# Split-precision products: high and low activations as one 512-wide moving operand, a PSUM bank per output chunk

## The chip, the core and the metric

The kernel runs on one core of one Trainium2 chip. The metric is device time in microseconds (us) of one execution. The kernel before takes 1823.14 us (median of three runs, 1821.18 to 1823.35).

## What is computed

The reference runs a stack of layers on x, 256 tokens by 1024 features, in float32. Two hybrid layers come first; each has five branches (stick-breaking attention, a matrix LSTM, spatial gating, retention, attention over a memory) that are projected up, gated and merged. Then come a recurrent mixer, a conformer convolution, two cross-attentions and two convolutional feed-forward blocks (FFN). What matters here is that nearly all the arithmetic is products of activations with large weight matrices that are read once from HBM:

```python
h = rms_norm(x, norm_pre)
proj = h @ w_in
...
h = rms_norm_2(x, norm) @ w_up
g = causal_dwconv(h[..., :D_FF], dw_w, dw_b)
u = h[..., D_FF:]
return (jax.nn.gelu(g) * u) @ w_down
```

The results have to be accurate to float32, while TensorE multiplies in a reduced format at full rate. So each operand is split into a high and a low part, and a product is the sum of three: high by high, high by low, low by high.

## The kernel before, in words

**Layout.** Most activations stand with features on the 128 partitions and the 256 tokens along the free axis; `xF` holds x as 8 chunks of 128 features. Other tensors stand with tokens on partitions ("row-major" below: `mm_T`, `proj_T`, `T_plain`, tile `psT`).

**Weights.** `weights` (L281) reads a block of weights as tiles `raw` of 1024 elements a partition, issued on SP's queue. ScalarE (ACT) writes the high part `wh` (L297), VectorE (DVE) the low part `wl` as raw minus high (L298). There are 5 buffers for `raw` and 4 for each split part, so the splits can run at most four tiles ahead of TensorE (PE). The two splits are given a priority ahead of the program order (`AHEAD`), and a scheduler writes out one fixed order for each engine. Every engine works through its order and waits where an operand or a buffer is missing.

**Products with features on partitions.** `Operand` (L244) holds the activations as two tiles, `h` and `l`. `mm_F` (L301) takes a block of 512 by 512 weights, and for each chunk of 128 outputs and each of four steps of 128 inputs it issues three matmuls of 256 columns, all into the same half of a PSUM bank:

```python
for n, (a, b) in enumerate(((wh, xh), (wh, xl), (wl, xh))):
    PE.matmul(pss[m // 2][:, m % 2], a, b,
```

`proj_F` (L328) makes 512 outputs of 1024 inputs with two such calls, into two banks of two chunks each. `scaled_F` (L344) then evicts a bank with one DVE multiplication by the row of reciprocal norms (`rb`), 512 elements wide:

```python
V.tensor_tensor(dst[:, 2 * i:2 * i + 2], pss[i], bc(rb, 2), op=ALU.mult)
```

The output products (tile `psO`) of the mixer, the conformer and the cross-attentions use four banks for all 8 chunks. The loop over input blocks is outside, that over the two column blocks of 512 inside, and `add_to_x` (L937) adds a bank to `xF` and makes the next stage's operand from it. Each hybrid layer's `w_out` product does the same and evicts through ACT (L878). The FFN's down product, `down` in `conv_ffn`, runs `mm_F` too.

**PSUM.** The pool `mm` has four banks for products, `aux` four for everything else; from its second block of 512 features on, the FFN's up projections take theirs from `aux`. Banks are handed out in turn, and a product waits until the bank's former contents have been read.

**Row-major products.** `mm_T` (L313) uses the activations as stationary operand and 512 columns of weights as moving one, again three matmuls a step.

Of the kernel before, what the change touches and what calls it, by code (L numbers as in the profile page):

```python
# [54 lines left out]
def stack_kernel(ctx: ExitStack, tc: tile.TileContext, I: dict, out: bass.AP):  # L55
# [245 lines left out]

    def mm_F(pss, src, op, k0, n_k, first, last):

        w = made.pop() if made else weights(src, n_k)
# [39 lines left out]
    def scaled_F(pss, rb, dst):  # L344

        for i in range(2):
            V.tensor_tensor(dst[:, 2 * i:2 * i + 2], pss[i], bc(rb, 2), op=ALU.mult)

    def F_plain(w, c0, op, rb, name, dst=None, pss=None):
        if pss is None:  # L350
            pss = proj_F(w, c0, op)
        if dst is None:
            dst = t_f4([128, 4, S], name)
        scaled_F(pss, rb, dst)
        return dst
# [9 lines left out]
    def silu2_F(w, c0, op, rb, name, pss=None):  # L365

        z = F_plain(w, c0, op, rb, name, pss=pss)
# [115 lines left out]
    def layer(l, nrm, early, kv, late, nxt):  # L483
# [3 lines left out]
        pss_q = proj_F(w, OFF["sb_q"], op)  # L487
        stage("layer")
        rc, row = nrm.column(), []
        pss_k = proj_F(w, OFF["sb_k"], op, mid=lambda: row.append(row_of(rc, "x")))  # L490
# [25 lines left out]
        def sb_branch():  # L516
            qF = F_plain(w, OFF["sb_q"], op, rb, "sbq", pss=pss_q)
            kF = F_plain(w, OFF["sb_k"], op, rb, "sbk", pss=pss_k)
# [36 lines left out]
            pss_z = proj_F(w, OFF["sb_z"], op, mid=later)  # L555
            z = silu2_F(w, OFF["sb_z"], op, rb, "sbz", pss=pss_z)
# [145 lines left out]
        def rt_branch():  # L702
# [5 lines left out]
            def rot(c0, name):  # L708
                pss = proj_F(w, c0, op)
                q = t_f4([128, 4, S], name)  # L710
                x = t_f4([128, 4, S], name + "_x")
                for i in range(2):
                    sl = slice(2 * i, 2 * i + 2)
                    V.tensor_tensor(q[:, sl], pss[i], bc(cr, 2), op=ALU.mult)
                    V.tensor_tensor(x[0:64, sl], pss[i][64:128], bc(sr[64:128], 2), op=ALU.mult)
                    V.tensor_tensor(x[64:128, sl], pss[i][0:64], bc(sr[0:64], 2), op=ALU.mult)
# [149 lines left out]
        pss = [[mbank([128, 2, S], "psO") for _ in range(2)] for _ in range(2)]  # L866
        for dh in range(2):
            for cg in range(2):
                mm_F(pss[cg], wo[dh * 512:dh * 512 + 512, cg * 512:cg * 512 + 512], mos[dh], 0, 4,
                     dh == 0, dh == 1)  # L870
        oF = [t_f4([128, 4, S], "oF") for _ in range(2)]
        sq = Sq()
        for cg in range(2):
            for i in range(2):
                sl = slice(2 * i, 2 * i + 2)
                for j in range(2):
                    c = 4 * cg + 2 * i + j
                    A.activation(oF[cg][:, 2 * i + j], pss[cg][i][:, j], AF.Copy,  # L878
                                 scale=col("norm_post", l * 8 + c))
                sq.add(pss[cg][i])  # L880
# [56 lines left out]
    def add_to_x(pss, nn, bias=None):  # L937
        for c2 in range(4):
            sl = slice(2 * c2, 2 * c2 + 2)
            ps = pss[c2 // 2][c2 % 2]  # L940
            if bias is None:
                V.tensor_tensor(xF[:, sl], xF[:, sl], ps, op=ALU.add)
            else:
                for j in range(2):
                    c = 2 * c2 + j
                    V.scalar_tensor_tensor(xF[:, c], ps[:, j], col(bias, c), xF[:, c],
                                           op0=ALU.add, op1=ALU.add)
            nn.pair(c2)
        return nn
# [17 lines left out]
    def mixer_ab(nrm, fill_1, fill_2, nxt):  # L967
# [3 lines left out]
        firsts = [proj_F(w, D, op)]  # L971
        rc, row = nrm.column(), []
        firsts.append(proj_F(w, D + 512, op, mid=lambda: row.append(row_of(rc, "x"))))
# [6 lines left out]
        def recurrence(g4):  # L980
            zr = F_plain(w, D + g4 * 512, op, rb, "a_zr", pss=firsts[g4])
# [39 lines left out]
        pss = proj_F(w, 2 * D, op)  # L1021
# [4 lines left out]
        up = t_f6([128, 4, 16 + S], "b_u")  # L1026
        G.memset(up[:, :, 0:16], 0.0)
        for i in range(2):
            V.tensor_tensor(up[:, 2 * i:2 * i + 2, 16:16 + S], pss[i], bc(rb, 2), op=ALU.mult)
# [32 lines left out]
        wo = I["ab_w_out_2"][0]  # L1062
        pss = out_banks()
        for n, (o, r0) in enumerate(((yb, D), (yas[0], 0), (yas[1], 512))):
            for cg in range(2):
                mm_F(pss[cg], wo[r0:r0 + 512, cg * 512:cg * 512 + 512], o, 0, 4, n == 0, n == 2)
        return add_to_x(pss, Norm(*nxt))

    def conformer(nrm, fill_1, fill_2, nxt):
# [3 lines left out]
        first = proj_F(w1, D, op, n=256)[0]  # L1073
# [337 lines left out]
```

## Time and profile before

| what | value |
|---|---|
| median of three runs | 1823.14 us |
| profiled execution | 1826.32 us |
| its span, first to last instruction | 1824.6 us |
| PE busy, matmuls | 1788.9 us (98%) |
| DVE busy | 1265.6 us (69%) |
| ACT busy | 958.9 us (53%) |
| mean granted TensorE clock | 0.993 |
| mean HBM traffic | 169 GB/s |

The profiled execution takes 1826.32 us, 1.7 us more than its span, and is 3.2 us above the median of the runs. In rows by group, the number after x is the count; after the bar come busy time in us, the mean of one in ns, and the engine's idle time just before such instructions with what ended it. In rows by window, the stretch and its length are followed by the busy time and count of PE, PEld (weight loads), DVE, ACT and POOL, then the granted clock as a share of full speed, the busy share of the DMA engines and GB/s. Timeline rows give the start, the duration, the engine and line, and in brackets the idle time before. In the rows of DMA queues the numbers are packets, MB and the share of 16 engines' time. A matmul's own duration includes its way through the array, and successive ones overlap, so rates are read from the distance between starts.

### The profile page before, as it was taken

The page shows a single profiled execution, that of the slowest core. Times are in us where ns is not written, and L with a number is a line of the kernel's source. Part 1 is how long each engine was busy: PE and PEld are TensorE (multiplying, and loading weights), DVE is VectorE, ACT ScalarE, POOL GpSimd, SP SyncE. Part 2 cuts the span into 40 slices and gives each one's busy share as a digit, 9 for nine tenths or more (in the row PEclk, how much of TensorE's full clock was granted, in tenths as well). Part 3 has the DMA queues.
Part 4 walks back from the last instruction along what each step waited for, and adds up shares of the span by engine and source line. Part 5 has one row for each costly group of instructions (what it writes and reads, how often), then busy time and mean ns, then how long its engine had stood idle before and what let it go on. Part 6 is the DMA issues. An engine that isn't in the chain of part 4 may idle for free. (4 is left out here: it accounts for less than half of the span.)

```text
span 1824.6 us, 30483 instructions
## 1 busy us (share of the span) xinstructions
PE 1788.9 (98%) x12255; PEld 1666.0 (91%) x12255; DVE 1265.6 (69%) x1888; ACT 958.9 (53%) x1369; POOL 60.8 (3%) x91
## 2 busy tenths in 40 slices
PE   8899999999999999999999999999999989999998
PEld 8889998888999898888899998999999989899998
DVE  6587856676667877656657965676669985577666
ACT  5755335554556443455455854455457545455443
POOL 0000001100000100000000000000000000000000
PEclk9999999999999999999999999999999999999999
DMA  7456554666554655467655554455554344355552
GB/s 222 131 167 208 168 174 147 202 206 193 165 173 146 185 176 169 149 197 232 207 169 178 156 169 144 155 181 178 183 183 146 103 133 151 116 180 184 183 184 93
DMA packets 162654, 309.57 MB, mean 170 GB/s; under 512 B 10852, under 2 KB 19504, under 8 KB 162512
## 3 DMA queue, kind: packets, MB, share of 16 engines
q1 hardware_dynamic: 159872, 302.04, 52.7%
q0 software_dynamic: 2128, 5.37, 1.0%
q8 instruction: 96, 1.57, 0.4%
q14 instruction: 46, 0.38, 0.1%
q10 hardware_dynamic: 512, 0.21, 0.1%
HBM read 306.53 MB, written 1.05 MB: 169 GB/s over the span
## 5 line engine op out<-in xcount | busy, mean ns | idle before, releaser
L298 DVE TENSOR_TENSOR wl<-raw,wh 128x1024 fp32r<-128x1024 f32 x558 | 668.6, 1222 | 343.8 <-ACT wh L297 335.4
L297 ACT ACTIVATE wh<-raw 128x1024 fp32r<-128x1024 f32 x558 | 573.2, 1054 | 529.9 <-PE psF L310 178.4
L310 PE MATMUL psF<-xh,wh 128*128 128x256 f32 x1888 | 538.4, 285 | 3.5 <-ACT wh L1302 3.3
L310 PE MATMUL psF<-xh,wl 128*128 128x256 f32 x1888 | 536.1, 284 | 0.8 <-DVE wl L298 0.8
L310 PE MATMUL psF<-xl,wh 128*128 128x256 f32 x1888 | 536.7, 284 | 0.0
L310 PEld LDWEIGHTS psF<-xh,wh 128*128 128x128 f32 x1888 | 363.7, 193 | 4.5 <-ACT wh L1302 3.6
L310 PEld LDWEIGHTS psF<-xl,wh 128*128 128x128 f32 x1888 | 364.0, 193 | 1.5 <-issue 1.0
L310 PEld LDWEIGHTS psF<-xh,wl 128*128 128x128 f32 x1888 | 363.3, 193 | 1.6 <-DVE wl L298 1.4
L310 PE MATMUL psO<-yh,wh 128*128 128x256 f32 x800 | 227.6, 285 | 6.0 <-ACT yh L253 6.0
L310 PE MATMUL psO<-yl,wh 128*128 128x256 f32 x800 | 227.3, 284 | 0.0
L310 PE MATMUL psO<-yh,wl 128*128 128x256 f32 x800 | 227.0, 284 | 0.3 <-DVE wl L298 0.3
L323 PE MATMUL psT<-wl,xh 128*128 128x512 f32 x544 | 216.3, 398 | 0.0
L323 PE MATMUL psT<-wh,xl 128*128 128x512 f32 x544 | 216.0, 397 | 0.0
L323 PE MATMUL psT<-wh,xh 128*128 128x512 f32 x544 | 214.5, 394 | 0.0
L310 PEld LDWEIGHTS psO<-yh,wh 128*128 128x128 f32 x800 | 154.2, 193 | 6.9 <-ACT yh L253 6.7
L310 PEld LDWEIGHTS psO<-yh,wl 128*128 128x128 f32 x800 | 154.3, 193 | 0.5 <-DVE wl L298 0.5
L310 PEld LDWEIGHTS psO<-yl,wh 128*128 128x128 f32 x800 | 154.3, 193 | 0.3
L323 PEld LDWEIGHTS psT<-wl,xh 128*128 128x128 f32 x544 | 102.7, 189 | 21.4
L323 PEld LDWEIGHTS psT<-wh,xl 128*128 128x128 f32 x544 | 102.8, 189 | 20.8
L323 PEld LDWEIGHTS psT<-wh,xh 128*128 128x128 f32 x544 | 102.8, 189 | 19.6
L1114 DVE SCALAR_TENSOR_TENSOR c_h<-c_a,cols,c_h 128x229 f32<-128x229 f32 (+15 forms) x144 | 63.2, 465 | 3.0
L323 PE MATMUL psT<-wl,yh 128*128 128x512 f32 x160 | 62.3, 389 | 0.0
(414 smaller groups left out, 2134.0 us busy)
## 6 DMA issues: line engine op xcount, KB each, us to landing
raw<-in_w_in SPq DMA_DIRECT2D x224, 512.0 KB, 4.3
raw<-in_f_w_up SPq DMA_DIRECT2D x96, 512.0 KB, 4.3
raw<-in_f_w_down SPq DMA_DIRECT2D x48, 512.0 KB, 4.3
raw<-in_w_up SPq DMA_DIRECT2D x40, 512.0 KB, 4.0
raw<-in_c_w_pw SPq DMA_DIRECT2D x24, 512.0 KB, 3.9
raw<-in_ab_w_in SPq DMA_DIRECT2D x20, 512.0 KB, 4.4
raw<-in_w_mem_kv SPq DMA_DIRECT2D x16, 512.0 KB, 3.9
raw<-in_w_out SPq DMA_DIRECT2D x16, 512.0 KB, 3.6
```

The source lines that it names most:

```text
L297: A.activation(hi, raw, AF.Copy)
L298: V.tensor_tensor(lo, raw, hi.bitcast(F32), op=ALU.subtract)
L310: PE.matmul(pss[m // 2][:, m % 2], a, b, start=(first and m % 2 == 0 and k == 0 and n == 0), stop=(last and k == n_k - 1 and n == 2), skip ...
L323: PE.matmul(pss[t], a, b, start=(first and k == 0 and n == 0), stop=(last and k == n_k - 1 and n == 2), skip_group_check=True)
L1114: V.scalar_tensor_tensor(h[:, j:], a[:, m, 0:S - j], col("c_dw_w_2", (30 - j) * 8 + c), h[:, j:], op0=ALU.mult, op1=ALU.add)
```

## The change

**Operand.** High and low parts stand side by side in one tile `hl`; `h` and `l` are views of it. `mm_P`, new, takes a block of 512 inputs by 256 outputs. For each step it issues two matmuls in place of three: the high weights against high and low activations as one moving operand of 512 columns, which fills a bank, and the low weights against the high activations, 256 columns added to the bank's first half. A bank holds one chunk of 128 outputs, and its halves are added at eviction.

**Eviction.** `join` copies the first half to SBUF on ACT and adds the second on DVE. `proj_F` makes its outputs by columns, 256 at a time over all 1024 inputs, and returns an SBUF tile; the multiplication by `rb` then reads and writes that tile. `proj_out` makes the output products in two halves of 512 columns, four banks each, and hands on two chunks at a time; `out_to_x` adds both halves of a bank to `xF` by two DVE instructions a chunk. `mm_F` stays for the FFN's down product alone. The weight tiles of the changed products are 4 by 256 elements a partition in place of 2 by 512: the same count and size, with runs of 1 KB in place of 2 KB.

```diff
-            self.h = pool.tile([128, n, S], F32R, tag=tag + "h", name=tag + "h")
-            self.l = pool.tile([128, n, S], F32R, tag=tag + "l", name=tag + "l")
+            self.hl = pool.tile([128, n, 2, S], F32R, tag=tag + "hl", name=tag + "hl")
+            self.h, self.l = self.hl[:, :, 0], self.hl[:, :, 1]
...
+    def mm_P(pss, src, op, k0, n_k, first, last):
+
+        w = made.pop() if made else weights(src, n_k)
+        for m in range(src.shape[1] // 128):
+            for k in range(n_k):
+                wh, wl = w[k][0][:, m * 128:m * 128 + 128], w[k][1][:, m * 128:m * 128 + 128]
+                PE.matmul(pss[m], wh, op.hl[:, k0 + k], start=(first and k == 0), stop=False,
+                          skip_group_check=True)
+                PE.matmul(pss[m][:, 0], wl, op.h[:, k0 + k], start=False,
+                          stop=(last and k == n_k - 1), skip_group_check=True)
...
-    def proj_F(w, c0, op, n_k=8, n=512, mid=None, get=None):
-        pss = [(get or mbank)([128, 2, S], "psF") for _ in range(n // 256)]
-        for k0 in range(0, n_k, 4):
-            if k0 and mid:
+    def join(dst, ps):
+        A.activation(dst, ps[:, 0], AF.Copy)
+        V.tensor_tensor(dst, dst, ps[:, 1], op=ALU.add)
+
+    def proj_F(w, c0, op, dst, n=512, mid=None, get=None):
+
+        for g in range(n // 256):
+            pss = [(get or mbank)([128, 2, S], "psF") for _ in range(2)]
+            for k0 in (0, 4):
+                mm_P(pss, w[k0 * 128:(k0 + 4) * 128, c0 + g * 256:c0 + g * 256 + 256], op, k0, 4,
+                     k0 == 0, k0 == 4)
+            for m in range(2):
+                join(dst[:, 2 * g + m], pss[m])
+            if mid and g == 0:
                 mid()
-            mm_F(pss, w[k0 * 128:(k0 + 4) * 128, c0:c0 + n], op, k0, 4, k0 == 0,
-                 k0 + 4 >= n_k)
-        return pss
+        return dst
+
+    def proj_out(w, parts, done):
+
+        for half in range(2):
+            banks = [[mbank([128, 2, S], "psO") for _ in range(2)] for _ in range(2)]
+            for n, (o, r0) in enumerate(parts):
+                for g in range(2):
+                    c0 = half * 512 + g * 256
+                    mm_P(banks[g], w[r0:r0 + 512, c0:c0 + 256], o, 0, 4, n == 0,
+                         n == len(parts) - 1)
+            for g in range(2):
+                done(2 * half + g, banks[g])
...
+    def out_to_x(w, parts, nn, bias=None):
+        def done(c2, banks):
+            for j in range(2):
+                c = 2 * c2 + j
+                if bias is None:
+                    V.tensor_tensor(xF[:, c], xF[:, c], banks[j][:, 0], op=ALU.add)
+                else:
+                    V.scalar_tensor_tensor(xF[:, c], banks[j][:, 0], col(bias, c), xF[:, c],
                                            op0=ALU.add, op1=ALU.add)
+                V.tensor_tensor(xF[:, c], xF[:, c], banks[j][:, 1], op=ALU.add)
             nn.pair(c2)
+
+        proj_out(w, parts, done)
```

The callers follow this. The first one or two projections of a stage now go to SBUF before the row `rb` exists. `w_out` evicts a chunk by `join`, then squares it and scales it in place on ACT. `rot` in the retention branch reads its swapped halves from SBUF. The first two weight blocks of the program are split in the new shape.

**ACT in the FFN**, one block of 512 hidden features in steady state. `f_gx` and `f_u` are the two up projections, `f_g` the gate, `wh` the high parts of weights, `yh` and `yhl` the operand of the down product. Before:

```order
L297 ACTIVATE wh<-raw 128x1024 x6
L388 ACTIVATE f_g<-f_gx,cols 128x256 x2
L297 ACTIVATE wh<-raw 128x1024 x2
L1223 ACTIVATE f_g<-f_g,cols 128x256 x2
L388 ACTIVATE f_g<-f_gx,cols 128x256 x2
L1223 ACTIVATE f_g<-f_g,cols 128x256 x2
L297 ACTIVATE wh<-raw 128x1024 x2
L253 ACTIVATE yh<-f_u 128x512
```

In the changed kernel:

```order
L297 ACTIVATE wh<-raw 128x1024 x5
L340 ACTIVATE f_gx<-psF 128x256
L297 ACTIVATE wh<-raw 128x1024
L340 ACTIVATE f_gx<-psF 128x256
L297 ACTIVATE wh<-raw 128x1024
L340 ACTIVATE f_gx<-psF 128x256
L297 ACTIVATE wh<-raw 128x1024
L340 ACTIVATE f_gx<-psF 128x256
L297 ACTIVATE wh<-raw 128x1024
L340 ACTIVATE f_u<-psF 128x256
```

Each eviction is now an ACT instruction that waits for PE, and one split of weights stands between two of them.

**PE at the conformer's end.** `ps_mean` is the mean over features for its layer norm, which waits for the last depthwise tap on DVE. `psF` is the second cross-attention's key projection, `psT` its value projection, `ps_ss` the sum of squares, `psO` the conformer's output product. Before:

```order
L310 MATMUL psF_14767<-mh_13658,wh_14836 128x256
L310 MATMUL psF_14767<-ml_13659,wh_14836 128x256
L310 MATMUL psF_14767<-mh_13658,wl_14837 128x256
L1124 MATMUL ps_mean_14894<-c_acc_14890,tri_ones_99 128x256 x2
L323 MATMUL psT_14952<-wh_14956,mh_13658 128x512
L323 MATMUL psT_14952<-wh_14956,ml_13659 128x512
L323 MATMUL psT_14952<-wl_14957,mh_13658 128x512
```

In the changed kernel:

```order
L334 MATMUL psT_13578<-wl_13618,mhl_12419 128x512
L1154 MATMUL ps_mean_13521<-c_acc_13517,tri_ones_99 128x256 x2
L334 MATMUL psT_13578<-wh_13617,mhl_12419 128x512 x2
L334 MATMUL psT_13578<-wl_13618,mhl_12419 128x512
L334 MATMUL psT_13578<-wh_13623,mhl_12419 128x512 x2
L334 MATMUL psT_13578<-wl_13624,mhl_12419 128x512
L334 MATMUL psT_13578<-wh_13623,mhl_12419 128x512 x2
L334 MATMUL psT_13578<-wl_13624,mhl_12419 128x512
L181 MATMUL ps_ss_13543<-tri_ones_99,sqacc_13526 128x1 x2
L194 MATMUL ps_rb_13549<-ident_91,cln_rc_13546 128x128 x2
L308 MATMUL psO_13655<-yhl_13554,wh_13661 128x512
```

Before, all 48 row-major matmuls of that projection stand behind the mean and 42 of them ahead of the sum of squares; now 39 stand ahead of the mean and 9 between the two sums.

**DVE at the same place.** `c_h` are the depthwise results, `c_acc` their sum over features, `kF` the keys. Before:

```order
L1114 SCALAR_TENSOR_TENSOR c_h<-c_a,cols,c_h 128x226
L1121 TENSOR_TENSOR c_acc<-c_acc,c_h 128x512
L298 TENSOR_TENSOR wl<-raw,wh 128x1024 x2
L347 TENSOR_TENSOR kF<-psF,mem_rb 128x512 x2
L298 TENSOR_TENSOR wl<-raw,wh 128x1024 x2
L1131 TENSOR_TENSOR c_h<-c_h,c_mean 128x512 x4
L232 TENSOR_TENSOR sqacc<-sqacc,sq 128x512
```

In the changed kernel:

```order
L341 TENSOR_TENSOR kF<-kF,psF 128x256
L1144 SCALAR_TENSOR_TENSOR c_h<-c_a,cols,c_h 128x229
L379 TENSOR_TENSOR kF<-kF,mem_rb 128x512
L1144 SCALAR_TENSOR_TENSOR c_h<-c_a,cols,c_h 128x228
L379 TENSOR_TENSOR kF<-kF,mem_rb 128x512
L1144 SCALAR_TENSOR_TENSOR c_h<-c_a,cols,c_h 128x227
L298 TENSOR_TENSOR wl<-raw,wh 128x1024
L1144 SCALAR_TENSOR_TENSOR c_h<-c_a,cols,c_h 128x226
L298 TENSOR_TENSOR wl<-raw,wh 128x1024
L1151 TENSOR_TENSOR c_acc<-c_acc,c_h 128x512
L1161 TENSOR_TENSOR c_h<-c_h,c_mean 128x512 x4
L232 TENSOR_TENSOR sqacc<-sqacc,sq 128x512
```

The eight key evictions, their scalings and the splits for the value projection now stand ahead of the last sum.

## Rows read from the trace of the kernel before

**Rows 1.** The page, busy time by engine, share of the span and instructions.

```profile
PE 1788.9 (98%) x12255; PEld 1666.0 (91%) x12255; DVE 1265.6 (69%) x1888; ACT 958.9 (53%) x1369; POOL 60.8 (3%) x91
```

**Rows 2.** Groups on PE: xcount, then busy us, mean ns, idle before.

```profile
L310 PE MATMUL psF<-xh,wh 128*128 128x256 f32 x1888 | 538.4, 285 | 3.5 <-ACT wh L1302 3.3 <-DVE a_z L347 0.2
...
L310 PE MATMUL psO<-yh,wh 128*128 128x256 f32 x800 | 227.6, 285 | 6.0 <-ACT yh L253 6.0
...
L310 PE MATMUL psF<-mh,wh 128*128 128x256 f32 x192 | 54.6, 284 | 0.0
```

**Rows 3.** PE timeline in a row-major stretch: start us, duration us.

```profile
900.15 0.39 PE L323 MATMUL psT<-wl,yh 128*128 128x512 f32 x1
...
903.55 0.39 PE L323 MATMUL psT<-wl,yh 128*128 128x512 f32 x1
```

**Rows 4.** Chain of waits, one unbroken run of features-first products.

```profile
1181.20 28.79 PE psF L310 x240
```

**Rows 5.** Busy by window: PE, PEld, DVE, ACT, POOL, granted clock, DMA, GB/s.

```profile
300.00:350.00 50.00, 50.00 (x222) 41.39 (x221) 29.14 (x29) 24.91 (x27) 12.28 (x24) 1.00 0.67 196
...
1200.00:1250.00 50.00, 50.00 (x419) 50.00 (x418) 35.16 (x45) 24.77 (x36) 0.00 (x0) 1.00 0.56 182
```

**Rows 6.** Groups on DVE and ACT by shape: what an eviction or split costs.

```profile
L298 DVE TENSOR_TENSOR wl<-raw,wh 128x1024 fp32r<-128x1024 f32 x558 | 668.6, 1222 | 343.8 <-ACT wh L297 335.4 <-PE ps_num L659 0.6
...
L942 DVE TENSOR_TENSOR xF<-xF,psO 128x512 f32<-128x512 f32 x20 | 13.7, 685 | 8.6 <-PE psO L310 8.6
...
L235 DVE TENSOR_TENSOR sqacc<-sqacc,sq 128x256 f32<-128x256 f32 x12 | 5.1, 421 | 0.2
...
L946 DVE SCALAR_TENSOR_TENSOR xF<-psO,cols,xF 128x256 f32<-128x256 f32 x8 | 3.8, 480 | 1.2 <-PE psO L310 1.2
...
L297 ACT ACTIVATE wh<-raw 128x1024 fp32r<-128x1024 f32 x558 | 573.2, 1054 | 529.9 <-PE psF L310 178.4 <-PE psT L323 161.6 <-issue 107.2
...
L878 ACT ACTIVATE oF<-psO,cols 128x256 f32<-128x256 f32 x16 | 6.6, 465 | 4.4 <-PE psO L310 4.4
...
L197 ACT ACTIVATE x_rb<-ps_rb 128x256 f32<-128x256 f32 x8 | 3.0, 369 | 2.6 <-PE ps_rb L194 2.6
```

**Rows 7.** Busy by window, the conformer's depthwise stage and its end.

```profile
1400.00:1450.00 50.00, 49.34 (x336) 47.50 (x335) 48.27 (x98) 30.53 (x77) 0.00 (x0) 1.00 0.27 85
1450.00:1500.00 50.00, 48.18 (x321) 44.77 (x319) 46.13 (x83) 21.59 (x36) 0.70 (x1) 1.00 0.42 137
```

**Rows 8.** DVE timeline at the conformer's end: last accumulate, idle gap.

```profile
1482.66 0.69 DVE L1121 TENSOR_TENSOR c_acc<-c_acc,c_h 128x512 f32<-128x512 f32 x1
...
1488.15 0.69 DVE L347 TENSOR_TENSOR kF<-psF,mem_rb 128x512 f32<-128x512 f32 x1 [1.93 <-PE psF L310]
```

**Rows 9.** PE timeline there: mean, sum of squares, first output product.

```profile
1487.95 1.03 PE L1124 MATMUL ps_mean<-c_acc,tri_ones 128*128 128x256 f32 x4
...
1498.39 0.61 PE L181 MATMUL ps_ss<-tri_ones,sqacc 128*128 128x1 f32 x4
...
1506.61 1.01 PE L310 MATMUL psO<-yh,wh 128*128 128x256 f32 x3 [4.95 <-ACT yh L253]
```

**Rows 10.** Busy by window around that idle stretch, with granted clock.

```profile
1500.00:1505.00 5.00, 1.64 (x8) 1.12 (x8) 4.35 (x6) 3.85 (x6) 0.00 (x0) 0.93 0.34 113
1505.00:1510.00 5.00, 3.39 (x14) 3.23 (x15) 1.79 (x3) 5.00 (x11) 0.00 (x0) 0.50 0.30 105
```

**Rows 11.** Busy by window, the recurrent mixer's second half.

```profile
1000.00:1050.00 50.00, 49.30 (x343) 45.94 (x341) 44.80 (x65) 44.12 (x58) 0.80 (x1) 1.00 0.48 152
```

**Rows 12.** What PE waited for: total us, times, longest.

```profile
PE psO L310 <- ACT yh L253: 6.0, 2, 4.9
...
PE psF L310 <- DVE wl L298: 0.8, 2, 0.5
```

**Rows 13.** DMA queue in 1380 to 1470, then in 1180 to 1350 us.

```profile
q1 hardware_dynamic: 6806, 9.54, 32.7%
...
q1 hardware_dynamic: 15950, 30.74, 55.8%
```

More of the change, by code (lines that the diff above doesn't have):

```diff
@@ L865, in layer @@
         wo = I["w_out"][l]
[L866 to L870, printed above, removed]
         oF = [t_f4([128, 4, S], "oF") for _ in range(2)]
         sq = Sq()
[L873 to L880, printed above, removed]
+        def done(c2, banks):
+            o2 = oF[c2 // 2][:, 2 * (c2 % 2):2 * (c2 % 2) + 2]
+            for j in range(2):
+                join(o2[:, j], banks[j])
+            sq.add(o2)
+            for j in range(2):
+                A.activation(o2[:, j], o2[:, j], AF.Copy,
+                             scale=col("norm_post", l * 8 + 2 * c2 + j))
+        proj_out(wo, [(mos[dh], dh * 512) for dh in range(2)], done)
         prb = row_of(sq.column("post"), "post")
@@ L935, in out_banks, with add_to_x, done @@
         return [[mbank([128, 2, S], "psO") for _ in range(2)] for _ in range(2)]
-    def add_to_x(pss, nn, bias=None):
+    def add_to_x(pss, nn):
         for c2 in range(4):
             sl = slice(2 * c2, 2 * c2 + 2)
[L940 to L946, printed above, removed]
+            V.tensor_tensor(xF[:, sl], xF[:, sl], pss[c2 // 2][c2 % 2], op=ALU.add)
+            nn.pair(c2)
+        return nn
+    def out_to_x(w, parts, nn, bias=None):
+        def done(c2, banks):
+            for j in range(2):
+                c = 2 * c2 + j
[3 more added lines that the diff above has]
+                    V.scalar_tensor_tensor(xF[:, c], banks[j][:, 0], col(bias, c), xF[:, c],
                                            op0=ALU.add, op1=ALU.add)
+                V.tensor_tensor(xF[:, c], xF[:, c], banks[j][:, 1], op=ALU.add)
             nn.pair(c2)
+        proj_out(w, parts, done)
         return nn
@@ L1061, in mixer_ab @@
         fill_2()
[L1062 to L1067, printed above, removed]
+        return out_to_x(I["ab_w_out_2"][0], [(yb, D), (yas[0], 0), (yas[1], 512)], Norm(*nxt))
     def conformer(nrm, fill_1, fill_2, nxt):
@@ L1072, in conformer @@
         stage("conf")
-        first = proj_F(w1, D, op, n=256)[0]
+        first = proj_F(w1, D, op, t_r1([128, 2, S], "c_g"), n=256)
         rc, row = nrm.column(), []
-        second = proj_F(w1, 0, op, n=256, mid=lambda: row.append(row_of(rc, "x")))[0]
+        second = proj_F(w1, 0, op, t_r1([128, 2, S], "c_a"), n=256,
+                        mid=lambda: row.append(row_of(rc, "x")))
         rb = row[0]
@@ L1158, in cross_attn @@
         stage("xa")
-        first = proj_F(wq, 0, op)
+        first = proj_F(wq, 0, op, t_f4([128, 4, S], "xq"))
         rc, row = nrm.column(), []
-        second = proj_F(wq, 512, op, mid=lambda: row.append(row_of(rc, "x")))
+        second = proj_F(wq, 512, op, t_f4([128, 4, S], "xq"), mid=lambda: row.append(row_of(rc, "x")))
         rb = row[0]
-        qF = [F_plain(wq, 0, op, rb, "xq", pss=first)]
+        qF = [F_plain(wq, 0, op, rb, "xq", raw=first)]
         def logits(h):
@@ L1298, in split @@
         def split(k):
-            hi = whl.tile([128, 2, 512], F32R, tag="wh", name="wh")
-            lo = whl.tile([128, 2, 512], F32R, tag="wl", name="wl")
-            for j in range(2):
-                A.activation(hi[:, j], raws[k][:, j], AF.Copy)
-                V.tensor_tensor(lo[:, j], raws[k][:, j], hi[:, j].bitcast(F32), op=ALU.subtract)
-            return [(hi[:, j], lo[:, j]) for j in range(2)]
+            hi = whl.tile([128, 4, 256], F32R, tag="wh", name="wh")
+            lo = whl.tile([128, 4, 256], F32R, tag="wl", name="wl")
+            for j in range(0, 4, 2):
+                sl = slice(j, j + 2)
+                A.activation(hi[:, sl], raws[k][:, sl], AF.Copy)
+                V.tensor_tensor(lo[:, sl], raws[k][:, sl], hi[:, sl].bitcast(F32), op=ALU.subtract)
+            made.insert(0, [(hi[:, j], lo[:, j]) for j in range(4)])
         def kept(c2):
@@ L1311, in stack_kernel @@
         turned(1)
+        split(0)
         turned(2)
-        parts = split(0)
         turned(3)
-        parts += split(1)
-        made.append(parts)
+        split(1)
         for c2 in range(4):
```

101 lines of the change are left out of this document (43 added, 58 removed).

## The prediction

> **What bounds the kernel now.** I read the page first: PE is busy for 98% of the span, DVE for 69%, ACT for 53% [rows 1]. An average hides stages, so the table by window comes next: in the FFN PE is busy for 50.00 us of 50 at full clock, with DVE at 35 and ACT at 25 [rows 5], while in the conformer DVE takes 48.27 of 50 [rows 7] and in the recurrent mixer's second half DVE and ACT take 44.80 and 44.12 [rows 11]. The list of waits confirms it: PE lost 6.0 us to the operand of output products, 4.9 of that in one place, and 0.8 us to late weight splits [rows 12]. So time is set by the rate of matmuls nearly everywhere, and by DVE's chains in two stretches.
>
> **The matmuls.** The rate is read from distances between starts. In an unbroken run of products with features on partitions, 240 matmuls take 28.79 us, 0.1200 us each for 256 columns [rows 4]. In a row-major stretch the first and last of 16 matmuls start 3.40 us apart, 0.2267 us each for 512 columns [rows 3]. The difference, 0.1067 us, is 256 columns at 2.4 GHz; so at either width 0.0133 us is paid for the instruction whatever its width. Three narrow ones cost 0.3599 us a product, one wide and one narrow one 0.3466: the change saves 0.0133 us a product.
>
> How many? A third of the matmuls: 1888 and 192 into `psF`, 800 into `psO` [rows 2]. The down products stay as they are: 2 layers x 6 blocks x 2 column blocks x 4 chunks x 4 steps = 384. That leaves 1888 + 192 + 416 = 2496, and the gain is 2496 x 0.0133 = **33.2 us** where PE is the bound. No row shows a wide matmul right behind a narrow one. Bounds from the nearest rows: the pair takes no less than its columns, 768 at 2.4 GHz = 0.3200 us, and, if the fixed part of three instructions stayed, 0.3599. I take 0.3466, since the two widths that the trace shows pay the same fixed part each.
>
> The Trainium skill, page "TensorE: Matmul & The Clock Gate", section "Back-to-back issue gap", speaks against a gain of this size: it gives a warm matmul its columns at 2.4 GHz and about 2.5 ns. By that one instruction less is worth 2.5 ns, and the sum would be 2496 x 2.5 ns = 6.2 us. The rows show 13.3 ns at both widths, so the rows decide.
>
> **The evictions.** 2080 products / 8 steps = 260 chunks go through `join`, and 16 more in the two `w_out`. ACT's copy of 128x256 out of PSUM costs between 0.369 and 0.465 us; I take 0.369, the row with a plain copy. DVE's add costs 0.421 (an add of this size in SBUF) to 0.480 (a three-operand form from PSUM); I take 0.421, as at 512 elements DVE is no slower from PSUM: 0.685 [rows 6]. So DVE gets 276 x 0.421 = 116 us. The additions to `xF` become 56 of 0.421 and 8 of 0.480, 27.4 us, in place of 12 at 0.685 and 8 at 0.480, 12.1 us: 15 us more. DVE comes to about 1397 us of some 1810, ACT to 959 + 276 x 0.369 = 1061. Neither becomes the bound on average.
>
> In the FFN the cover holds. A block of 512 hidden features takes some 34 us on PE; eight joins add 3.4 us on DVE, and 35.16 of 50 becomes about 40 [rows 5]. A bank must be read when its pool comes round, two groups of two chunks later: one group between, 16 x 0.3466 = 5.5 us, plus the first chunk's head start of 1.4. The join needs 0.8 us and at worst a split ahead of it on each queue, 1.05 and 1.22 [rows 6]. The order of ACT shows just one split between two joins. The splits lose nothing: a tile now serves 8 products at a stretch, and three more may be ready behind it.
>
> **What is lost.**
> - *Conformer.* Its depthwise stage runs at DVE's pace: 94.4 us busy in 100 [rows 7]. It gets 16 joins of its own and, by the order, eight key joins ahead of the last accumulation, 24 x 0.421 = 10.1 us. The free time that could take them is at most 5.6 us, of which one gap is 1.93 [rows 8], so the sum of squares comes 4.5 to 10.1 us later; I take 7. The order also moves 39 of 48 row-major matmuls ahead of the mean. Where 10.4 us between mean and sum of squares were filled [rows 9], PE will now stand idle for most of them; that moves idle time and is not counted again. The saving on the 192 products in there, 2.6 us, is not collected since DVE sets the pace. Together 9.6.
> - *Recurrent mixer.* About 11 joins fall in its last 50 us, 4.8 us on DVE and 4.2 on ACT, where the chain goes back and forth between the two and leaves 5 to 6 us free on each [rows 11]. Between 0 and 9 us; I take 4, and 1 for savings not collected.
> - *Branches of the hybrid layers.* DVE bunches there, and some joins will come late. Nothing in the trace shows this wait; between 0, as in the FFN, and one 1.22 us split at six or seven places, 8 us. I take 3.
> - *Stage ends.* After the last output product come two adds, the copy and the split of the last chunks: 0.84 + 0.5 + 0.5 us and the hand-overs, against 2.8 us of cover by the next stage's first tile. 0 to 1.5 us at four places; I take 2 in all.
> - *DMA.* Runs of 1 KB instead of 2 KB cost nothing: where more than half of the traffic is such reads, 9.54 MB in 90 us take 32.7% of the queues' time, and 30.74 MB in 170 us take 55.8% [rows 13]; per MB that is 3.08 and 3.09 us.
>
> Sum: 33.2 - 9.6 - 5 - 3 - 2 = 13.6 us less. Against the profiled execution's 1826.3 us that is 1812.7; that execution lies 3.2 above the median, so I forecast **1809.5 us** for the median.
>
> **Rivals.**
> 1. *Everything is covered.* DVE's free time takes the joins in the conformer (4.5 us late, not 7), and the mixer, branches and stage ends lose nothing: 33.2 - 7.1 = 26, or 1797 us. For it: the queues run three weight tiles ahead of PE, so that short delays vanish. Against: DVE's share in [rows 7]. Chance 0.13.
> 2. *The losses take up the gain.* All upper bounds at once: 12.7 + 10 + 8 + 6 = 36.7, or 1826.6; any loss between 30 and 37 us ends within 0.2% of the time before. Chance 0.11.
> 3. *Slower: banks come free too late.* Two chunks now fill two banks where two held four, and each needs both ACT and DVE. Where DVE's queue is more than 6 us behind (five splits of 1.22), PE stops at a hand-over. Of 260 chunks 164 lie outside the FFN, 82 groups. If a third of them overrun by one split of 1.22 us, that is 33 us, or 1843; eleven overruns eat the forecast gain. For it: DVE near full in [rows 7] and [rows 11]. Against: in most branches DVE has room, and a join does not wait for the row of norms. Chance 0.06. What a stop costs beyond its length, the rows show: after 4.95 us without work the granted clock was 0.50 for 5 us [rows 9, 10]. The same page of the Trainium skill, section "A second HAM failure mode: psum-queue depth-cycling", tells of a kernel with 512-wide matmuls whose cycling through banks left PE short idle times often enough that its clock fell and rose. The row-major stretch, which hands over a bank every 24 x 0.2267 = 5.4 us, holds 1.00 [rows 5]; after the change it is one every 2.8 us.
> 4. *The pair is no faster than the three.* If a wide matmul behind a narrow one still pays three fixed parts, 0.3599 us a product, nothing is gained and the losses stay, less the 3.6 us of savings counted as not collected: 16 us, or 1839. Against: [rows 3, 4]. Chance 0.04. The section on the issue gap, named above, would leave 6.2 us of gain and so come out at about 1833.
>
> **Chances.** The forecast, with losses between 8 and 29 us around the 19.6 taken, has 0.66. A run of this kernel is told from no change by about 0.2%, 3.6 us: under 1819.5 is faster, over 1826.8 slower. Faster has 0.66 + 0.13 = 0.79, about the same 0.11, slower 0.06 + 0.04 = 0.10. The range for 8 in 10 goes from rival 1 to the top of rival 2: 1796 to 1826.
>
> **What would show it.** In the profile after, runs of 16 matmuls into `psF` should take 2.77 us (0.3466 a pair); 0.360 speaks for rival 4. In the FFN windows PE should stay at 50 of 50 with DVE near 40, and the list of waits should show no DVE or ACT join ahead of `psF`; many such waits in the branches mean rival 3. At the conformer's end PE should idle some 10 us or more between the mean and the first output product, and the step from first depthwise tap to that product should grow by about 7 us less what PE saves before. The forecast is wrong if the idle time of PE grows by more than 29 us, or if the conformer and the mixer do not grow at all.

## The result: 0.7% slower, and the profile after

Medians of four runs of each kernel:

| | before | after |
|---|---|---|
| median of the runs | 1822.49 us | 1836.22 us |
| ratio, 95% interval | | 1.0072, 1.0054 to 1.0089 |
| span of the profiled execution | 1824.6 us | 1834.5 us |
| mean granted TensorE clock | 0.993 | 0.987 |

1809.5 was forecast, with 1796 to 1826 as the range: the sign was wrong. The page of the changed kernel, busy time by engine [rows 1]:

```profile
PE 1776.3 (97%) x9759; PEld 1534.4 (84%) x9759; DVE 1374.2 (75%) x2208; ACT 1053.8 (57%) x1645; POOL 56.1 (3%) x91
```

The 2496 matmuls are gone, but PE is busy for only 12.6 us less, and it stands idle for 1834.5 - 1776.3 = 58.2 us where it stood for 35.7, so the span grows by 9.9. DVE and ACT have about the work that the prediction gave them (1397 and 1061).

PE's groups [rows 2], then its timeline in the first FFN, four starts of wide matmuls:

```profile
L308 PE MATMUL psF<-xhl,wh 128*128 128x512 f32 x1888 | 673.7, 400 | 11.2 <-DVE fa L212 4.3 <-DVE sbq L341 2.9 <-DVE rtq L341 1.2
L310 PE MATMUL psF<-xhl,wl 128*128 128x256 f32 x1888 | 531.0, 282 | 1.1 <-DVE wl L298 1.1
...
L308 PE MATMUL psO<-yhl,wh 128*128 128x512 f32 x416 | 149.6, 403 | 4.7 <-DVE yhl L254 4.7
```
```profile
1202.86 0.39 PE L308 MATMUL psF<-xhl,wh 128*128 128x512 f32 x1
...
1208.41 0.39 PE L308 MATMUL psF<-xhl,wh 128*128 128x512 f32 x1
...
1266.88 0.40 PE L308 MATMUL psF<-xhl,wh 128*128 128x512 f32 x1
...
1273.95 0.40 PE L308 MATMUL psF<-xhl,wh 128*128 128x512 f32 x1
```

Between the first two lie 16 pairs, 5.55 us: 0.3469 a pair, as predicted. Between the last two lie 20, 7.07 us: 0.3535. An unbroken run mostly keeps one of the two lengths to its end; of about 240 stretches of eight pairs at full clock 61 had the short one. The long one saves 0.0064 us a product, half of the 0.0133.

Busy time by window (PE, PEld, DVE, ACT, POOL, clock), against [rows 5, 7, 11]:

```profile
1000.00:1050.00 50.00, 44.81 (x242) 37.26 (x240) 45.97 (x72) 46.10 (x71) 0.76 (x1) 0.98 0.53 162
...
1200.00:1250.00 50.00, 50.00 (x318) 45.20 (x317) 41.22 (x63) 31.80 (x52) 0.00 (x0) 1.00 0.60 186
...
1450.00:1500.00 50.00, 48.11 (x246) 42.52 (x245) 47.58 (x99) 26.62 (x65) 0.00 (x0) 0.97 0.32 102
1500.00:1550.00 50.00, 38.62 (x193) 32.61 (x192) 35.81 (x59) 28.75 (x44) 0.69 (x1) 0.86 0.38 120
```

The FFN is what was forecast: PE without a gap, DVE at 41. In the mixer's second half PE has lost 4.5 us more than before, and around the conformer's end 11.4 of 50. What PE waited for [rows 12], total us, times, longest:

```profile
PE ps_pool L1088 <- ACT a_z L340: 6.3, 1, 6.3
PE ps_ss L181 <- DVE sqacc L235: 5.6, 1, 5.6
PE psO L308 <- DVE yhl L254: 4.7, 1, 4.7
PE psF L308 <- DVE fa L212: 4.3, 1, 4.3
PE psT L334 <- DVE mlk_x L341: 3.5, 2, 1.8
PE psF L308 <- DVE sbq L341: 2.9, 1, 2.9
...
PE psF L308 <- DVE rtq L341: 1.2, 1, 1.2
```

Four of the seven name a join (L340, L341), and the fourth row is one too, under another name. The timeline there, in layer 0:

```profile
87.97 0.38 ACT L340 ACTIVATE mlq_x<-psF 128x256 f32<-128x256 f32 x1
...
90.66 0.28 PE L310 MATMUL psF<-xhl,wl 128*128 128x256 f32 x1
95.25 0.54 PE L308 MATMUL psF<-xhl,wh 128*128 128x512 f32 x1 [4.31 <-DVE fa L212]
...
95.81 0.63 PE L308 MATMUL psF<-xhl,wh 128*128 128x512 f32 x1
...
96.45 0.63 PE L308 MATMUL psF<-xhl,wh 128*128 128x512 f32 x1
...
93.48 1.22 DVE L298 TENSOR_TENSOR wl<-raw,wh 128x1024 fp32r<-128x1024 f32 x1
94.62 0.16 DVE L211 TENSOR_TENSOR sp_r<-sp_e 128x8 f32<-128x8 f32 x1
94.69 0.41 DVE L341 TENSOR_TENSOR mlq_x<-mlq_x,psF 128x256 f32<-128x256 f32 x1
```

ACT copied the first of four chunks at 87.97. Its add stood in DVE's fixed order behind splits and small chains and ran at 94.69, more than six microseconds later; four chunks fill the four banks of `mm`, so the fifth could start only then. After this stop the matmuls run at half speed for a while: the next pairs start 0.64 us apart, and the granted clock is 0.66 over 95 to 100 us. Nor is this join alone. From the end of a copy to the end of its add pass 2.05 us on average over the 276 joins, and over 4 us for 42 of them. In all the mean clock makes (1 - 0.987) x 2 x 1834.5 = 48 us at the lower of the two levels, 1.2 GHz, against 26 before.

### The profile page after: what moved, and what is told of

Its sections match the earlier page's. It is cut to its first block, busy times and chain, and to the rows that moved or that the text cites. A ratio compares the mean times of both kernels' runs of the same rounds, so it can differ in the third digit from the quotient of the medians.

```text
span 1834.5 us, 26140 instructions
## 1 busy us (share of the span) xinstructions
PE 1776.3 (97%) x9759; PEld 1534.4 (84%) x9759; DVE 1374.2 (75%) x2208; ACT 1053.8 (57%) x1645; POOL 56.1 (3%) x91
## 4 chain that ended last, share of the span: by engine, by line
PE 70%; issue 18%; DVE 7%; ACT 3%; DMA 1%; POOL 0%; DVEq 0%; POOLq 0%; ACTq 0%
PE psT L334 25%; PE psF L308 18%; PE psF L310 9%; PE psO L308 5%; PE psO L321 4%; PE psO L310 2%; DVE wl L298 2%; DVE c_h L1144 2%; PE ps_lg L925 1%; PE ps_conv L1133 1%; ACT wh L297 1%; PE ps_blk L435 1%; PE ps_xo L1210 1%; DMA raw<-in_w_in 1%; PE ps_xo L858 0%
## 5 line engine op out<-in xcount | busy, mean ns | idle before, releaser
L308 PE MATMUL psF<-xhl,wh 128*128 128x512 f32 x1888 | 673.7, 400 | 11.2 <-DVE fa L212 4.3
L310 PE MATMUL psF<-xhl,wl 128*128 128x256 f32 x1888 | 531.0, 282 | 1.1 <-DVE wl L298 1.1
L308 PEld LDWEIGHTS psF<-xhl,wh 128*128 128x128 f32 x1888 | 356.2, 189 | 96.5 <-issue 9.6
L310 PEld LDWEIGHTS psF<-xhl,wl 128*128 128x128 f32 x1888 | 358.6, 190 | 4.9 <-DVE wl L298 2.8
L334 PE MATMUL psT<-wh,xhl 128*128 128x512 f32 x1088 | 342.8, 394 | 3.5 <-DVE mlk_x L341 3.5
L334 PEld LDWEIGHTS psT<-wh,xhl 128*128 128x128 f32 x1088 | 203.2, 188 | 44.4 <-issue 4.1
L334 PE MATMUL psT<-wl,xhl 128*128 128x512 f32 x544 | 215.6, 396 | 0.0
L321 PEld LDWEIGHTS psO<-yhl,wh 128*128 128x128 f32 x768 | 118.7, 189 | 0.4
L310 PE MATMUL psO<-yhl,wl 128*128 128x256 f32 x416 | 117.5, 283 | 0.0
L321 PE MATMUL psO<-yhl,wl 128*128 128x256 f32 x384 | 108.8, 283 | 0.0
L308 PEld LDWEIGHTS psO<-yhl,wh 128*128 128x128 f32 x416 | 79.1, 190 | 24.5 <-issue 5.7
L310 PEld LDWEIGHTS psO<-yhl,wl 128*128 128x128 f32 x416 | 79.7, 192 | 0.2
L321 PEld LDWEIGHTS psO<-yhl,wl 128*128 128x128 f32 x384 | 72.6, 189 | 0.0
```

What stands on the lines that cost most here:

```text
L308: PE.matmul(pss[m], wh, op.hl[:, k0 + k], start=(first and k == 0), stop=False, skip_group_check=True)
L310: PE.matmul(pss[m][:, 0], wl, op.h[:, k0 + k], start=False, stop=(last and k == n_k - 1), skip_group_check=True)
L321: PE.matmul(pss[m // 2][:, m % 2], a, b, start=(first and m % 2 == 0 and k == 0 and n == 0), stop=(last and k == n_k - 1 and n == 2), skip ...
L334: PE.matmul(pss[t], a, b, start=(first and k == 0 and n == 0), stop=(last and k == n_k - 1 and n == 2), skip_group_check=True)
```

## Experiments

**Which part costs.** Four runs split the change. Without the second half, high weights by low x is computed and not added. The other three hold the whole computation.

```diff
 # e3_no_second_half: join, and the same in out_to_x
-        V.tensor_tensor(dst, dst, ps[:, 1], op=ALU.add)
 # e2_three_narrow: mm_P
-                PE.matmul(pss[m], wh, op.hl[:, k0 + k], ...)
+                PE.matmul(pss[m][:, 0], wh, op.h[:, k0 + k], ...)
+                PE.matmul(pss[m][:, 1], wh, op.l[:, k0 + k], ...)
 # e10_no_join_narrow: as e2, all three into pss[m][:, 0], and no add
 # e4_one_reduce: join
-        A.activation(dst, ps[:, 0], AF.Copy)
-        V.tensor_tensor(dst, dst, ps[:, 1], op=ALU.add)
+        V.tensor_reduce(dst, ps.rearrange("p a b -> p b a"), axis=AX.X, op=ALU.add)
```

> The addition of the bank's second half is left out everywhere (276 adds on DVE of about 0.42 us, and 32 into the residual): the product of the high weights with low x is computed and not used. ACT's copy, the order by columns and the weight tiles stay. Theory 'late evictions, on DVE': DVE gets back some 130 us, PE's idle time falls to near that of the kernel before, and the time goes to 1803 to 1815. Rival 'ACT's hop or the order by columns and the tiles of 256 columns are what costs': 1830 to 1836.

> The products go back to three matmuls of width 256 (the second into the other half of the chunk's bank); evictions, the order by columns and the weight tiles stay as changed. It splits the loss into what the wide matmul gives and what the rest takes. Theory 'late evictions' (the wide matmul gives 2496 x 0.009 = 23 us, and the copies and adds take about 37): 1854 to 1859. Rival 'the wide matmul gives nearly nothing, for PE waits anyway where it would gain': 1836 to 1842, and then the rest takes only 14 to 20.

> Order by columns, weight tiles of 256 columns, one chunk a bank and ACT's copy as in the change, but three narrow matmuls into the one half, so that no add is wanted. What is left against the kernel before is the price of order, tiles, a bank a chunk and the copy; what is left against the run without the second half (1804) is the worth of the wide matmul where no add stands in its way. Theory 'DVE's work': within 5 of the kernel before, 1821 to 1827, so that the wide matmul is worth 17 to 23 here and the rest of the change costs little. Rival 'order, tiles and copy cost as well': 1832 to 1840.

> The changed kernel with each join as one DVE reduction over the two halves of the bank instead of ACT's copy and DVE's add. DVE reads 512 elements instead of 256: by the 512-element eviction of the kernel before (0.685 us) that is 0.26 us more for each of 276 joins, 73 us in all; ACT loses 276 copies of 0.37, 102 us, and the chain from bank to tile loses one hop between engines. Theory 'DVE's work' (the loss of the change is the time that DVE's adds take in stretches where DVE sets the pace; 116 us of adds cost 32): the further 73 us cost 15 to 25, 1851 to 1861. Rival 'length of the chain' (the loss is the hop from ACT to DVE, not DVE's time): 1820 to 1832.

Measured: e3 1804.03 us (0.9901 of before, 0.9886 to 0.9916); e2 1850.07 (1.0156, 1.0142 to 1.0170); e10 1823.06 (0.9999, 0.9991 to 1.0008); e4 1834.83 (1.0069, 1.0056 to 1.0083). The pages of e3 and of e10:

```profile
PE 1766.7 (98%) x9759; PEld 1529.9 (85%) x9759; DVE 1271.3 (71%) x1900; ACT 1055.2 (59%) x1645; POOL 57.4 (3%) x91
```
```profile
PE 1789.9 (98%) x12255; PEld 1668.6 (92%) x12255; DVE 1272.9 (70%) x1900; ACT 1053.4 (58%) x1645; POOL 56.1 (3%) x91
```

The change closes in three steps. Order by columns, tiles of 256 columns, a bank a chunk and ACT's copy: nothing (e10 against before). The wide matmul: 1823.06 - 1804.03 = 19.0 us gained. The adds: 1836.22 - 1804.03 = 32.2 us lost (27.0 with three narrow ones, e2 - e10). The kernel before, run beside each, differed by up to 1 us between these runs, so each step is good to 1 or 2 us. With joins in the way the wide matmul keeps 13.9 of its 19.0 (e2 against the changed kernel); e2 fell between the two expectations. So DVE's adds turn the sign. But e4 speaks against DVE's time as the whole of it. Its page and one of its groups:

```profile
PE 1773.9 (97%) x9759; PEld 1533.2 (84%) x9759; DVE 1442.1 (79%) x2208; ACT 976.4 (53%) x1369; POOL 56.7 (3%) x91
```
```profile
L340 DVE TENSOR_REDUCE f_gx<-psF 128x256 f32<-128x512 f32 x48 | 32.7, 688 | 0.4
```

DVE has 68 us more to do than in the changed kernel, ACT 77 less, and the time is the same. Neither expectation fits. What e4 shortens is the time for which a bank is held: from a chunk's last matmul to the end of the instruction that frees the bank pass 3.65 us on average in the changed kernel, 3.19 in e4, and 1.5 where the copy alone frees it (e3, e10). The averages are over the 260 chunks in `psF`.

**Where.** The change was made in one stage at a time, or taken out of one.

> The kernel before, with the change made in the two hybrid layers alone (memory keys as before). In the profile of the changed kernel the two layers take 8 us more than before. Theory 'their own joins': 1828 to 1834, most of the whole loss. Rival 'brought along by the memory keys' joins': 1820 to 1825.

> The changed kernel with the six projections of memory keys (24 of 276 joined chunks; they fill PE's time inside other stages, two of them in the conformer) made as before: three narrow matmuls, no join. The conformer alone changed cost nothing, yet the conformer's stretch was 5.2 us longer in the changed kernel, so something that the other parts put there must do it. Theory 'the keys' joins crowd DVE where it sets the pace': the conformer's stretch falls back to 165 from 169.9 and the whole to 1828 to 1832. Rival 'the conformer's loss comes from somewhere else in the change': 1834 to 1838.

> The kernel before, with the change made in the recurrent mixer alone. In the profile of the changed kernel the mixer's stretch is 4.3 us longer than before and 10.2 us of it are at the half clock. Theory 'its own joins': 1825 to 1828. Rival 'brought along from other parts, as in the conformer': 1822, within 2.

> The kernel before, with the change made in the conformer alone (its gated projections and its output products). In the profile of the changed kernel the stretch from the conformer's row of norms to the next stage's row is 5.2 us longer than before, and 10.2 us more of it is at the half clock. Theory 'joins on DVE, and a clock that falls while PE waits': 4 to 7 us slower, 1826 to 1829, with 10 us or more at the half clock there. Rival 'the conformer's loss is brought along from the stages before it': 1822, within 2.

> The kernel before, with the change made in the FFN's two projections alone (768 of 2496 products); hybrid layers, mixer, conformer and cross attention keep three narrow matmuls and evictions without a join. Theory 'late evictions' (the FFN has room on DVE and ACT for the joins, and PE is busy throughout): the gain there is what a pair saves, 768 x 0.0066 to 0.0133 = 5 to 10 us, so 1812 to 1818. Rival 'the FFN gives nothing either': 1822, within 3.

| changed alone | us | against before |
|---|---|---|
| e14, hybrid layers | 1833.19 | 1.0055 (1.0043 to 1.0067), +10.5 |
| e13, mixer | 1826.96 | 1.0023 (1.0015 to 1.0032), +4.3 |
| e6, conformer | 1822.98 | 0.9998 (0.9989 to 1.0007), +0.3 |
| e5, FFN | 1816.08 | 0.9968 (0.9957 to 0.9980), -5.6 |
| e11, all but the memory keys | 1828.89 | 1.0026 (1.0016 to 1.0036); the keys thus +7.3 |

The layers and the mixer fit "their own joins", the conformer the rival's time, e5 and e11 the first theory. With 2.2 us gained in the cross attentions (e9, below, against e5; e9 also has another order of matmuls) the parts add up to +14.6; +13.7 was measured. The surprise is the conformer: its own joins cost nothing. The conformer's stretch, from the start of its row of norms in `ps_rb` to the next stage's, is 164.7 us before, 169.9 after, 165.3 with it alone changed, and 165.3 with everything but the keys. PE's waits in that stretch of e11:

```profile
PE psO L308 <- DVE yhl L254: 4.7, 1, 4.7
PE ps_ss L181 <- DVE sqacc L235: 2.7, 1, 2.7
```

The wait for the sum of squares is 2.7 us where it was 5.6. Key projections fill PE's time at the conformer's end, and their joins there delay what follows. The mixer's loss, on the other hand, is its own, at one place. PE's waits in e13, mixer alone:

```profile
PE ps_pool L1110 <- ACT a_z L348: 6.3, 1, 6.3
```

The same stop in the changed kernel, rows of three engines:

```profile
1050.27 1.19 ACT L340 ACTIVATE a_z<-psF 128x256 f32<-128x256 f32 x4
...
1051.54 0.15 DVE L1082 TENSOR_TENSOR b_p<-b_p,b_u 128x2 f32<-128x2 f32 x1
...
1051.79 1.84 PE L1088 MATMUL ps_pool<-b_p,b_gw 128*128 128x256 f32 x3 [6.30 <-ACT a_z L340]
...
1052.70 0.41 DVE L341 TENSOR_TENSOR a_z<-a_z,psF 128x256 f32<-128x256 f32 x1
```

The profile puts the wait down to ACT's copies of `a_z`, but these end at 1051.46. The product that starts then reads `b_p`, and DVE's last instruction on it ends at 1051.69: 55.0 us behind the start of the mixer's row of norms, where it was 49.4 before. PE has nothing else to put into the gap. The four copies of `a_z` stand in ACT's order behind the recurrence (its table load and its 1024-wide instructions), the adds stand in DVE's, and so all four product banks stay full. The first row-major product starts at 1053.50, after the first add. Before, the same four chunks filled two banks, and row-major products started as soon as those of `a_z` were done, at 1037.94. So a later chain on DVE and full banks come together here. e10, with the same banks and copies but no add, has no stop at `ps_pool`. How much is due to which isn't shown; a run with more banks for products wasn't made.

**By which mechanism an add costs.** Three runs; the first two rest on e10.

```diff
 # e12_dve_work_alone, behind the copy: nobody reads the result
+        V.tensor_tensor(ps[:, 1], ps[:, 0], unit, op=ALU.add)
 # e16_work_and_chain_no_bank, behind the copy: changes nothing, bank already free
+        V.tensor_tensor(dst, dst, dst, op=ALU.max)
 # e18_joins_first: the changed kernel's join
+        with tc.high_priority(offset=ahead[0]):
             A.activation(dst, ps[:, 0], AF.Copy)
             V.tensor_tensor(dst, dst, ps[:, 1], op=ALU.add)
```

> The kernel with order by columns and ACT's copy but three narrow matmuls into one half (1823), and behind each of 276 copies an addition on DVE of the size of the join's, out of the bank's first half into its unused second half, whose result nobody reads. It puts the join's work on DVE without putting it between the product and its reader. Theory 'DVE's time' (what the add takes from DVE's other instructions is the loss): most of the 27 us that lie between this kernel and the one with real joins (1850), so 1840 to 1850. Rival 'the chain' (the loss is the add's place between product and reader): 1823 to 1830.

> The kernel with order by columns, ACT's copy and three narrow matmuls into one half (1823), and behind each copy a DVE instruction of the join's size on the tile itself (the larger of the tile and itself, which changes nothing). It has the join's work on DVE and its place between product and reader, but the bank is free once ACT has copied. Theory 'banks held' (PE stops because a bank waits for an add that stands in DVE's queue): 1823 to 1832, though work and chain are as in the kernel with three narrow matmuls and real joins (1850). Rival 'DVE's time and the chain': 1843 to 1852.

> The changed kernel with the same instructions, but each join's copy and add are given the priority ahead of the program order that the weight splits have, so that the fixed orders of ACT and DVE put them earlier. Theory 'banks held': PE's stops at hand-overs shrink, and some 10 to 20 us of the loss come back, 1816 to 1828. Rival 'DVE's time' (the same work is only moved, and what it passes comes later): 1833 to 1842.

Measured: e12 1861.41 us (1.0207, 1.0194 to 1.0221), e16 1837.62 (1.0084, 1.0070 to 1.0097), e18 1818.76 (0.9981, 0.9973 to 0.9990). e16 lands between its expectations: work and place in the chain are worth 1837.62 - 1823.06 = 14.6 us. The other 1850.07 - 1837.62 = 12.4 go to holding the bank, together with the 32 adds of second halves to `xF`, which e2 has and e16 leaves out. e12's instruction took as long as an add:

```profile
L344 DVE TENSOR_TENSOR psF<-psF,tri_ones 128x256 f32<-128x256 f32 x260 | 108.9, 427 | 5.8 <-ACT sbz L343 2.2 <-ACT mlq_x L343 1.6 <-ACT xaq L343 0.6
```

and yet cost 38 us, more than a real add; both expectations missed. It holds the bank as well, so it doesn't isolate DVE's time as it was meant to: in its list of waits PE stops for 16.2 us at banks that these adds still hold. It doesn't come later than a real add either: 1.94 us on average from the end of the copy to its own end, against 1.84 in e2. Why it costs 11 us more than e2 stays open. e18 has the instructions of the changed kernel, the same busy time on DVE, and 17.5 us less, as 'banks held' expected:

```profile
PE 1765.0 (97%) x9759; PEld 1527.7 (84%) x9759; DVE 1374.1 (76%) x2208; ACT 1055.4 (58%) x1645; POOL 56.9 (3%) x91
```
```profile
PE ps_ss L181 <- DVE sqacc L235: 5.9, 1, 5.9
PE psT L334 <- DVE a_z L342: 5.7, 1, 5.7
PE psO L308 <- DVE yhl L254: 5.7, 2, 4.7
PE psF L310 <- DVE wl L298: 5.1, 2, 4.7
```

In its list of waits (the second of these fences) those for `fa`, `sbq` and `rtq` are gone and `mlk_x` is down to 0.5; the conformer's and the mixer's stay, and late splits of weights are new. From copy to add pass 1.03 us on average where it was 2.05, and over 4 us twice where it was 42 times; a bank is held for 2.34 us where it was 3.65. By the profiles the two hybrid layers end at 979.3 us in place of 996.7, so nearly all of the gain lies there. So more than half of the 32.2 us was where the joins stood in their queues, not how long they take. The copies were moved ahead together with the adds; what this does to a kernel without adds wasn't tried.

**The pair, and the best version.**

```diff
 # e1_four_and_four: mm_P
             for k in range(n_k):
                 PE.matmul(pss[m], wh, op.hl[:, k0 + k], ...)
+            for k in range(n_k):
                 PE.matmul(pss[m][:, 0], wl, op.h[:, k0 + k], ...)
 # e19: e18 with this; e9: FFN and cross attention alone with this
 # e20: layers with joins first; FFN, cross attention as changed; the rest as before
```

> After the change a pair of one wide and one narrow matmul takes 0.3514 us on average (0.2345 and 0.1170), not 0.3466. Here each chunk issues its four wide matmuls first and its four narrow ones behind them; nothing else changes. Theory 'alternation' (a change of width between neighbours is what costs the missing 0.0048 us a pair): four pairs take 4 x 0.3466 us, and the kernel gains up to 2496 x 0.0048 = 12 us, 1824 to 1828. Theory 'fixed' (the pair costs 0.3514 in whatever order): 1836, within 3.

> The run with joins first, and with four wide and then four narrow matmuls a chunk. That order took 7 us off the changed kernel. Theory: the two add, 1809 to 1823 where joins first give 1816 to 1828. Rival 'the order of four and four helped only because it freed banks in another rhythm, which joins first do already': within 3 of the run with joins first.

> The change made in the FFN's two projections and in the cross attention of its own stage (query and output products) alone, with four wide and then four narrow matmuls a chunk; all else as before. In the profile of the changed kernel these are the stages that got shorter: 3.1 and 2.8 us in the two FFNs, 1.1 and 0.8 in the two cross attentions, and the order of four and four took another 0.1 to 0.4 in each. Theory 'the change pays where PE sets the pace': 1812 to 1815. Rival 'the cross attention's gain came from elsewhere': as with the FFN alone, 1816.

> The change in the hybrid layers with joins first, in the cross attentions and the FFN with joins in program order, and not in the mixer, the conformer and the memory keys. In the profiles, joins first made the two layers 6 and 3 us shorter than before where the change alone made them 2 and 6 longer; the mixer stayed 4 us longer, and the conformer with the keys 2 to 5. Theory 'stages add up': the FFN and cross attention alone gave 1814 (with four wide and four narrow; 1814 to 1815 without), and the layers add 3 to 6, so 1808 to 1812. Rival 'the layers gained only because the later stages took over their work': 1814 to 1820.

Measured: e1 1828.8 us (1.0036, 1.0024 to 1.0049), e19 1820.27 (0.9985, 0.9976 to 0.9994), e9 1813.85 (0.9952, 0.9939 to 0.9964), e20 1814.38 (0.9949, 0.9934 to 0.9964). The timeline of e1 in the same FFN, each row four matmuls:

```profile
1266.09 1.09 PE L308 MATMUL psF<-xhl,wh 128*128 128x512 f32 x4
...
1277.31 1.09 PE L308 MATMUL psF<-xhl,wh 128*128 128x512 f32 x4
```

32 pairs in 11.22 us, 0.3506 each: about 0.003 less than the long pair, not 0.3466. The change of width between neighbours isn't what costs, and e1's time fits neither expectation. e1's gain doesn't lie in the FFN (201.3 and 197.7 us before it, 201.2 and 197.4 with it), and with joins first the order adds nothing (e19). e9 is 8.9 us faster than the kernel before; in e20 the layers with joins first add nothing more to this, as the rival had it. They take 979 us together in e18's profile, 989 in e20's, 985 in e9's, where they are as before. But e20's profiled execution took 1818.36 us, 4.0 above the median, and has 24 us of the layers at the lower clock where e18's has 7. PE idles for 20 us of them in both. So it isn't shown that the layers lose what e18 gave them; their clock differed.

## Why the prediction was wrong

Two terms of the sum carry the miss: the gain was put 14 us too high, and the loss in the hybrid layers some 14 us too low. With the gain alone put right the forecast would have been no change (19.0 against losses of 19.6); the loss made it slower. The sign that the prediction set itself, PE's idle time growing by more than 29 us, didn't show: it grew by 22.5, because part of the miss lies in PE's busy time.

- **33.2 us from the matmuls: mis-sized.** It is worth 19.0, 0.0076 us a product. "The two widths that the trace shows pay the same fixed part each" held for one of the two lengths of a pair; the bounds of 0.3200 to 0.3599 were right, but the sum's value stood at the better case. The sign of 2.77 us for 16 matmuls was met in the short runs alone.
- **Branches of the hybrid layers, 3 us with an end at 8: the step that failed.** Changed alone, the layers are 10.5 us slower. Of the 2496 products 832 are theirs, worth 6.3 us at 0.0076, so the loss there is near 17. "One 1.22 us split at six or seven places" priced a late join by the split ahead of it; the rows show whole chains ahead of it, and a stop of 4.3 us at one place. The same instructions with the joins first (e18) took the layers from 996.7 to 979.3 us.
- **Memory keys: only eight of 24 joined chunks had a price**, those in the conformer. Together they cost 7.3 us, of which 169.9 - 165.3 = 4.6 lie in the conformer's stretch.
- **Conformer, 9.6 us: right place, too much, and the wrong joins.** The stretch grew by 5.2, of which 4.6 go with the keys. PE does idle between mean and sum of squares as forecast, and the clock pays:

```profile
1503.98 1.02 PE L1154 MATMUL ps_mean<-c_acc,tri_ones 128*128 128x256 f32 x4
...
1512.74 1.02 PE L181 MATMUL ps_ss<-tri_ones,sqacc 128*128 128x1 f32 x4 [5.64 <-DVE sqacc L235]
...
1520.71 0.77 PE L308 MATMUL psO<-yhl,wh 128*128 128x512 f32 x1 [4.71 <-DVE yhl L254]
```

  Mean to first output product took 16.7 us where it took 18.7 [rows 9], so the idle time was indeed moved. "Not counted again" left out that PE now has two idle times there in place of one: the granted clock was 0.86 over 1500 to 1550, and 0.51 over 1512 to 1526.
- **Mixer, 5 us: right in size, not in kind.** Not many short delays on DVE and ACT, but one stop of 6.3 us, with `b_p` late on DVE and all product banks full.
- **Stage ends, 2 us: not measured by themselves.** No run has them alone.
- **FFN, DMA, averages: right.** PE 50.00 of 50, DVE 41.22; order and 1 KB runs cost nothing (e10).
- **Rival 3, chance 0.06, names the mechanism.** It asked for 27 short overruns. The list of waits names eight at joins, up to 6.3 us long (the one at `ps_pool`, a join's only in part) and 21 us together: a bank waits for the later of two engines, each with its own queue ahead. The argument against it, that "DVE has room" in the branches, reads an average of a window. That the rival's 1843 lies near the measured time is luck in part, since it still counts on 33.2 us of gain. The rule of the Trainium skill, page "TensorE: Matmul & The Clock Gate", section "Back-to-back issue gap", gave 6.2 us of gain; the page states it for an isolated matmul. The runs gave 19.0, so it is too low here.

What stays open: why a pair keeps one of two lengths; why a reduction with more DVE time cost no more than copy and add (a shorter hold, 3.19 against 3.65 us, fits with banks held, but its share wasn't measured by itself); why e12 cost more than e2; and how e16's 14.6 us split between DVE's time and the chain.

## What to carry to other kernels

A change that saves matmuls and pays at the eviction is priced by how long the banks stay full: count the banks that a group of products holds, and for each place where DVE or ACT runs a chain, look up what stands ahead of the eviction in its fixed order. Where evictions need two engines, give them priority before judging the change (17.5 us here), and apply it first to the stages in which PE alone sets the pace: the FFN and the cross attention gave 8.9 us (e9). Work that fills gaps of other stages, like the memory keys, brings its evictions along.

## What the runs showed that was not expected

A wide matmul and a narrow one in turn settle into 0.347 or 0.3535 us and mostly stay there until the run breaks. An added DVE instruction whose result is not read cost 38 us for 115.5 us of work (e12), more than one in the chain that holds no bank (e16, 14.6). That points to what it held rather than to who waited for it, but e12 also cost 11 us more than real joins on the same matmuls (e2), and this isn't explained.
